# RMSNorm with every row written twice: eight rows per partition in one load, each row normalised in place and stored by itself, all loads of x and all stores in SyncE's queue

## The chip, the cores and the metric

The kernel runs on one core of a Trainium2 chip. The metric is the device time of one execution in microseconds (us). The time of the kernel before is 245.04 us in the first three runs (244.88 to 245.27). The program uses VectorE (DVE), ScalarE (ACT), GpSimd (POOL), SyncE (SP) and the 16 DMA engines that serve the core. TensorE does nothing.

In a profile the "span" is the time from the first to the last instruction. The device time is 1.7 to 2.0 us longer in all runs of this study.

Some terms. "The page" is the profiler's summary of one execution, in numbered parts. An engine issues a transfer into a queue of its own; the 16 DMA engines carry it out in packets.

## The reference

```python
x: (8, 512, 2048) float32, gamma: (2048,) float32

x_rep = np.repeat(x, 2, axis=1)
rms = np.sqrt((x_rep ** 2).mean(axis=-1, keepdims=True) + 1e-6)
return (x_rep / rms) * gamma          # (8, 1024, 2048) float32
```

There are 4096 rows of 8 KB. Each is read once and written twice, next to each other: 33.6 MB in, 67.1 MB out, 100.7 MB in all.

## The kernel before

A tile is 256 rows: 128 partitions of two rows. The 16 tiles are loaded by SyncE as runs of 16 KB per partition. GpSimd issues two stores per tile, one for each copy. A store moves runs of 8 KB, with a gap of 8 KB between them in memory, where the other copy goes.

```python
K = 2
x_t = x_f.rearrange("(n p k) d -> n p k d", p=P, k=K)
out_t = out_v.rearrange("(n p k) r d -> n p k r d", p=P, k=K)
BUFS = 6                                   # for x_tile and for sq_tile
# ... gamma by SyncE, then broadcast to 128 partitions by GpSimd
for i in range(ntiles):
    x_tile = xin.tile([P, K, D], f32)
    nc.sync.dma_start(out=x_tile[:], in_=x_t[i])
    # ... ScalarE: square with row sums, square root; VectorE: reciprocal
    y_tile = sq_tile
    for k in range(K):
        nc.vector.tensor_scalar_mul(out=y_tile[:, k, :], in0=x_tile[:, k, :],
                                    scalar1=rstd[:, k : k + 1])
    nc.vector.tensor_mul(out=y_tile[:], in0=y_tile[:], in1=gamma_kd)
    for r in range(R):
        nc.gpsimd.dma_start(out=out_t[i, :, :, r, :], in_=y_tile[:])
```

Of the kernel before, what the change touches and what calls it, by code (L numbers as in the profile page):

```python
# [1 line left out]

# [4 lines left out]


@with_exitstack  # L10
def kernel(
    ctx: ExitStack,
    tc: tile.TileContext,
    x: bass.AP,
    gamma: bass.AP,
    out: bass.AP,
):
    nc = tc.nc
    P = nc.NUM_PARTITIONS

    B, S, D = x.shape
    Bo, So, Do = out.shape
    R = So // S
    assert D == Do and B == Bo and So == S * R
    eps = 1e-6

    x_f = x.rearrange("b s d -> (b s) d")
    N = B * S
    K = 2
    assert N % (P * K) == 0  # L30
    ntiles = N // (P * K)
    x_t = x_f.rearrange("(n p k) d -> n p k d", p=P, k=K)

    out_v = out.rearrange("b (s r) d -> (b s) r d", r=R)
    out_t = out_v.rearrange("(n p k) r d -> n p k r d", p=P, k=K)

    BUFS = 6
    singles = ctx.enter_context(tc.tile_pool(name="singles", bufs=1))
    xin = ctx.enter_context(tc.tile_pool(name="xin", bufs=BUFS))
    sq = ctx.enter_context(tc.tile_pool(name="sq", bufs=BUFS))  # L40
    small = ctx.enter_context(tc.tile_pool(name="small", bufs=8))

    gamma_b = singles.tile([P, D], mybir.dt.float32)
    nc.sync.dma_start(out=gamma_b[0:1, :], in_=gamma.partition_broadcast(1))
    nc.gpsimd.partition_broadcast(out_ap=gamma_b[:], in_ap=gamma_b[0:1, :])  # L45
    gamma_kd = bass.AP(
        tensor=gamma_b.tensor,
        offset=gamma_b.offset,
        ap=[gamma_b.ap[0], [0, K], gamma_b.ap[1]],
    )  # L50

    eps_t = singles.tile([P, 1], mybir.dt.float32)
    nc.vector.memset(eps_t, eps)  # L53

    inv_d = 1.0 / float(D)

    for i in range(ntiles):
        x_tile = xin.tile([P, K, D], mybir.dt.float32, name="x_tile")
        nc.sync.dma_start(out=x_tile[:], in_=x_t[i])

        sq_tile = sq.tile([P, K, D], mybir.dt.float32, name="sq_tile")
        ss = small.tile([P, K], mybir.dt.float32, name="ss")
        for k in range(K):
            nc.scalar.activation(  # L64
                out=sq_tile[:, k, :],
                in_=x_tile[:, k, :],
                func=mybir.ActivationFunctionType.Square,
                accum_out=ss[:, k : k + 1],
            )

        rms = small.tile([P, K], mybir.dt.float32, name="rms")
        nc.scalar.activation(  # L72
            out=rms[:],
            in_=ss[:],
            func=mybir.ActivationFunctionType.Sqrt,
            scale=inv_d,
            bias=eps_t[:],
        )
        rstd = small.tile([P, K], mybir.dt.float32, name="rstd")
        nc.vector.reciprocal(out=rstd[:], in_=rms[:])  # L80

        y_tile = sq_tile
        for k in range(K):
            nc.vector.tensor_scalar_mul(  # L84
                out=y_tile[:, k, :], in0=x_tile[:, k, :], scalar1=rstd[:, k : k + 1]
            )
        nc.vector.tensor_mul(out=y_tile[:], in0=y_tile[:], in1=gamma_kd)  # L87

        for r in range(R):
            nc.gpsimd.dma_start(out=out_t[i, :, :, r, :], in_=y_tile[:])  # L90


# [1 line left out]
_INS = ['x', 'gamma']  # L94
_OUTS = [((8, 1024, 2048), 'float32')]


# [23 lines left out]
```

## Time and profile before

Part 2 of the page of the kernel before: busy tenths in 40 equal slices of the span (9 is 90% or more), and under them what the DMA engines moved in each slice.

```profile
DVE  0069999950900049680095709577595600000000
ACT  2598656006000150600615061541624000000000
POOL 4003223411010101110130111111121111000000
DMA  6999999999999999999999999999999999999993
GB/s 222 431 431 431 391 433 429 436 417 442 422 431 430 433 422 431 429 427 430 425 430 450 410 426 426 430 425 430 429 425 418 418 417 419 430 417 425 417 426 160
```

The DMA row is 9 from the second slice to the last but one, at about 430 GB/s. No compute row is. A change of the compute can save nothing here unless it also changes what the DMA engines do, or when they start and stop.

Part 5 of the same page, the costliest groups: line, engine, operation, tiles and shapes, count, then busy us and mean ns of one, then the idle time before them with its releaser.

```profile
L64 ACT ACTIVATE sq_tile<-x_tile 128x2048 f32<-128x2048 f32 x32 | 60.8, 1901 | 114.1 <-DMA out_dram<-sq_tile 101.1
L87 DVE TENSOR_TENSOR sq_tile<-sq_tile,gamma_b 128x4096 f32<-128x4096 f32 x16 | 70.8, 4422 | 0.5
L90 POOL DMA_DIRECT2D out_dram<-sq_tile x32 | 27.7, 867 | 169.3 <-DMA out_dram<-sq_tile 125.6
L84 DVE TENSOR_SCALAR sq_tile<-x_tile,rstd 128x2048 f32<-128x2048 f32 x32 | 40.2, 1298 | 0.5
```

ScalarE and GpSimd idle because buffers and earlier stores have not come free: they wait for the DMA engines, not the other way round.

The trace also records every DMA packet with its queue, size, start and duration. At any time about 16 packets run in these records, one for each engine, so "per engine" below is the sum of all durations divided by 16. Durations in a table like this are sums and means over those records; "excess" is what a group of packets took above the median packet of its size.

| kernel before | value |
|---|---|
| first x packet starts | 2.10 us |
| 2048 load packets of 16 KB: median, mean, per engine | 611 ns, 622 ns, 79.6 us |
| 8192 store packets of 8 KB: median, mean, per engine | 309 ns, 311 ns, 159.3 us |
| last store packet ends | 240.57 us |
| span ends | 243.03 us |

This is the DMA row of the transfers between 236 and 246 us, in 40 slices of 0.25 us:

```profile
DMA  9899998999934533000000000000000000000000
```

The engines do not all stop together. The row falls from the twelfth slice on; the last packet ends at 240.57 us. The 16 landings of the last store are spread over 1.81 us. From the last packet to the end of the span there are another 2.46 us.

### The profile page before, as it was taken

The page shows a single profiled execution, that of the slowest core. Times are in us where ns is not written, and L with a number is a line of the kernel's source. Part 1 is how long each engine was busy: PE and PEld are TensorE (multiplying, and loading weights), DVE is VectorE, ACT ScalarE, POOL GpSimd, SP SyncE. Part 2 cuts the span into 40 slices and gives each one's busy share as a digit, 9 for nine tenths or more (in the row PEclk, how much of TensorE's full clock was granted, in tenths as well). Part 3 has the DMA queues.
Part 4 walks back from the last instruction along what each step waited for, and adds up shares of the span by engine and source line. Part 5 has one row for each costly group of instructions (what it writes and reads, how often), then busy time and mean ns, then how long its engine had stood idle before and what let it go on. Part 6 is the DMA issues. An engine that isn't in the chain of part 4 may idle for free.

```text
span 243.0 us, 320 instructions
## 1 busy us (share of the span) xinstructions
DVE 112.7 (46%) x65; ACT 69.5 (29%) x82; POOL 30.2 (12%) x37
## 2 busy tenths in 40 slices
DVE  0069999950900049680095709577595600000000
ACT  2598656006000150600615061541624000000000
POOL 4003223411010101110130111111121111000000
DMA  6999999999999999999999999999999999999993
GB/s 222 431 431 431 391 433 429 436 417 442 422 431 430 433 422 431 429 427 430 425 430 450 410 426 426 430 425 430 429 425 418 418 417 419 430 417 425 417 426 160
DMA packets 11012, 100.69 MB, mean 414 GB/s; under 512 B 769, under 2 KB 769, under 8 KB 769
## 3 DMA queue, kind: packets, MB, share of 16 engines
q0 software_dynamic: 8704, 67.11, 65.7%
q1 hardware_dynamic: 2306, 33.56, 32.8%
q14 instruction: 2, 0.02, 0.0%
HBM read 33.56 MB, written 67.11 MB: 414 GB/s over the span
## 4 chain that ended last, share of the span: by engine, by line
DMA 50%; another core or an unknown queue 15%; issue 4%; ACT 3%; DVE 2%; POOL 1%; POOLq 0%; ACTq 0%
DMA out_dram<-sq_tile 50%; ACT sq_tile L64 3%; DVE sq_tile L87 2%; POOL out_dram L90 1%; POOLq L116 0%; ACT rms L72 0%; DVE rstd L80 0%; ACTq L64 0%; POOLq L90 0%
## 5 line engine op out<-in xcount | busy, mean ns | idle before, releaser
L64 ACT ACTIVATE sq_tile<-x_tile 128x2048 f32<-128x2048 f32 x32 | 60.8, 1901 | 114.1 <-DMA out_dram<-sq_tile 101.1
L87 DVE TENSOR_TENSOR sq_tile<-sq_tile,gamma_b 128x4096 f32<-128x4096 f32 x16 | 70.8, 4422 | 0.5
L90 POOL DMA_DIRECT2D out_dram<-sq_tile x32 | 27.7, 867 | 169.3 <-DMA out_dram<-sq_tile 125.6
L84 DVE TENSOR_SCALAR sq_tile<-x_tile,rstd 128x2048 f32<-128x2048 f32 x32 | 40.2, 1298 | 0.5
L80 DVE RECIPROCAL rstd<-rms 128x2 f32<-128x2 f32 x16 | 2.6, 163 | 77.8 <-ACT rms L72 77.8
L64 ACT ACTIVATION_READ_ACCUMULATOR sq_tile<-x_tile 128x1 f32 x32 | 6.0, 186 | 0.0
L72 ACT ACTIVATE rms<-ss,eps_t 128x2 f32<-128x2 f32 x16 | 4.7, 296 | 0.5
L45 POOL PARTITION_BROADCAST gamma_b<-gamma_b x1 | 2.3, 2293 | 2.1 <-DMA gamma_b<-in_gamma_dram 2.1
L64 ACT ACT_TABLE_LOAD x1 | 1.3, 1283 | 0.7 <-PEq L105 0.7
L72 ACT ACT_TABLE_LOAD x1 | 1.3, 1283 | 0.0
L53 DVE MEMSET eps_t<- 128x1 f32 x1 | 0.1, 59 | 0.8 <-PEq L105 0.8
L105 POOL MEMSET const-float32-0.0<- 128x1 f32 x1 | 0.1, 99 | 0.2 <-issue 0.2
L105 POOL MEMSET const-uint8-127<- 128x1 uint8 x1 | 0.1, 103 | 0.0
L105 POOL MEMSET const-bfloat16-1.0<- 128x1 bf16 x1 | 0.1, 102 | 0.0
L105 POOL MEMSET const-float32-1.0<- 128x1 f32 x1 | 0.1, 99 | 0.0
## 6 DMA issues: line engine op xcount, KB each, us to landing
out_dram<-sq_tile POOLq DMA_DIRECT2D x32, 2048.0 KB, 40.7
x_tile<-in_x_dram SPq DMA_DIRECT2D x16, 2048.0 KB, 24.4
gamma_b<-in_gamma_dram SPq DMA_DIRECT2D x1, 8.0 KB
```

Source lines behind the costliest of these rows:

```text
L45: nc.gpsimd.partition_broadcast(out_ap=gamma_b[:], in_ap=gamma_b[0:1, :])
L53: nc.vector.memset(eps_t, eps)
L64: nc.scalar.activation(out=sq_tile[:, k, :], in_=x_tile[:, k, :], func=mybir.ActivationFunctionType.Square, accum_out=ss[:, k : k + 1],)
L72: nc.scalar.activation(out=rms[:], in_=ss[:], func=mybir.ActivationFunctionType.Sqrt, scale=inv_d, bias=eps_t[:],)
L80: nc.vector.reciprocal(out=rstd[:], in_=rms[:])
L84: nc.vector.tensor_scalar_mul(out=y_tile[:, k, :], in0=x_tile[:, k, :], scalar1=rstd[:, k : k + 1])
L87: nc.vector.tensor_mul(out=y_tile[:], in0=y_tile[:], in1=gamma_kd)
L90: nc.gpsimd.dma_start(out=out_t[i, :, :, r, :], in_=y_tile[:])
L105: nc = _bacc.Bacc("TRN2", target_bir_lowering=False, num_devices=1)
```

## The change

Its intent: fewer and longer load packets (eight rows, 64 KB, per partition); one fused VectorE operation in place, so that no second big buffer is needed; a store for each row as soon as it is ready, with both copies in one transfer, the source repeated by a step of zero; and no use of GpSimd's queue.

```diff
-    K = 2
+    K = 8
-    BUFS = 6
+    BUFS = 3
 ...        (also cut: the new views x_t and out_t, the list xs of loaded tiles)
+    def load(i, parts=1):
+        xt = xin.tile([P, K, D], f32, name="xt")
+        step = K // parts
+        for k in range(0, K, step):
+            nc.sync.dma_start(out=xt[:, k : k + step, :], in_=x_t[i, :, k : k + step, :])
+    def repeated(row):
+        p, d = row.ap
+        return bass.AP(tensor=row.tensor, offset=row.offset, ap=[p, [0, R], d])
+
+    load(0, parts=K // 2)
-    nc.sync.dma_start(out=gamma_b[0:1, :], in_=gamma.partition_broadcast(1))
+    nc.scalar.dma_start(out=gamma_b[0:1, :], in_=gamma.partition_broadcast(1))
 ...
+    for i in range(1, BUFS):
+        load(i)
     for i in range(ntiles):
 ...        (square and square root per row, the squares thrown away in PSUM)
-            nc.vector.tensor_scalar_mul(out=y_tile[:, k, :], in0=x_tile[:, k, :], ...)
-        nc.vector.tensor_mul(out=y_tile[:], in0=y_tile[:], in1=gamma_kd)
-        for r in range(R):
-            nc.gpsimd.dma_start(out=out_t[i, :, :, r, :], in_=y_tile[:])
+            nc.vector.scalar_tensor_tensor(
+                out=xt[:, k, :], in0=xt[:, k, :], scalar=rstd[:], in1=gamma_b[:],
+                op0=Alu.mult, op1=Alu.mult)
+            nc.sync.dma_start(out=out_t[i, :, k], in_=repeated(xt[:, k, :]))
+            if k == K // 2 and 1 <= i and i + BUFS - 1 < ntiles:
+                load(i + BUFS - 1)
```

There are now four tiles of 1024 rows. SyncE's program is: four loads of two rows, two loads of eight rows, 13 stores, the last load, 19 stores.

More of the change, by code (lines that the diff above doesn't have):

```diff
@@ L19 @@
     P = nc.NUM_PARTITIONS
+    f32 = mybir.dt.float32
+    Act = mybir.ActivationFunctionType
+    Alu = mybir.AluOpType
     B, S, D = x.shape
@@ L23 @@
     R = So // S
-    assert D == Do and B == Bo and So == S * R
+    assert R == 2 and D == Do and B == Bo and So == S * R
     eps = 1e-6
-    x_f = x.rearrange("b s d -> (b s) d")
+    inv_d = 1.0 / float(D)
+    K = 8
     N = B * S
-    K = 2
     assert N % (P * K) == 0
     ntiles = N // (P * K)
-    x_t = x_f.rearrange("(n p k) d -> n p k d", p=P, k=K)
-    out_v = out.rearrange("b (s r) d -> (b s) r d", r=R)
-    out_t = out_v.rearrange("(n p k) r d -> n p k r d", p=P, k=K)
-    BUFS = 6
+    x_t = x.rearrange("b s d -> (b s) d").rearrange("(n p k) d -> n p k d", p=P, k=K)
@@ L38 @@
+    out_t = out.rearrange("b s d -> (b s) d").rearrange("(n p k r) d -> n p k r d", p=P, k=K, r=R)
+    BUFS = 3
     singles = ctx.enter_context(tc.tile_pool(name="singles", bufs=1))
     xin = ctx.enter_context(tc.tile_pool(name="xin", bufs=BUFS))
-    sq = ctx.enter_context(tc.tile_pool(name="sq", bufs=BUFS))
+    junk = ctx.enter_context(tc.tile_pool(name="junk", bufs=1, space=bass.MemoryType.PSUM))
     small = ctx.enter_context(tc.tile_pool(name="small", bufs=8))
-    gamma_b = singles.tile([P, D], mybir.dt.float32)
@@ L44 @@
-    nc.sync.dma_start(out=gamma_b[0:1, :], in_=gamma.partition_broadcast(1))
-    nc.gpsimd.partition_broadcast(out_ap=gamma_b[:], in_ap=gamma_b[0:1, :])
-    gamma_kd = bass.AP(
-        tensor=gamma_b.tensor,
-        offset=gamma_b.offset,
-        ap=[gamma_b.ap[0], [0, K], gamma_b.ap[1]],
-    )
-    eps_t = singles.tile([P, 1], mybir.dt.float32)
+    xs = []
+    def load(i, parts=1):
[3 more added lines that the diff above has]
+            nc.sync.dma_start(out=xt[:, k : k + step, :], in_=x_t[i, :, k : k + step, :])
+        xs.append(xt)
@@ L53 @@
+    def repeated(row):
+        p, d = row.ap
+        return bass.AP(tensor=row.tensor, offset=row.offset, ap=[p, [0, R], d])
+    load(0, parts=K // 2)
+    gamma_b = singles.tile([P, D], f32, name="gamma_b")
+    nc.scalar.dma_start(out=gamma_b[0:1, :], in_=gamma.partition_broadcast(1))
+    nc.gpsimd.partition_broadcast(out_ap=gamma_b[:], in_ap=gamma_b[0:1, :])
+    eps_t = singles.tile([P, 1], f32, name="eps_t")
     nc.vector.memset(eps_t, eps)
-    inv_d = 1.0 / float(D)
+    for i in range(1, BUFS):
+        load(i)
@@ L57 @@
     for i in range(ntiles):
-        x_tile = xin.tile([P, K, D], mybir.dt.float32, name="x_tile")
-        nc.sync.dma_start(out=x_tile[:], in_=x_t[i])
-        sq_tile = sq.tile([P, K, D], mybir.dt.float32, name="sq_tile")
-        ss = small.tile([P, K], mybir.dt.float32, name="ss")
+        xt = xs[i]
         for k in range(K):
-            nc.scalar.activation(
-                out=sq_tile[:, k, :],
-                in_=x_tile[:, k, :],
-                func=mybir.ActivationFunctionType.Square,
-                accum_out=ss[:, k : k + 1],
-            )
@@ L71 @@
-        rms = small.tile([P, K], mybir.dt.float32, name="rms")
-        nc.scalar.activation(
-            out=rms[:],
-            in_=ss[:],
-            func=mybir.ActivationFunctionType.Sqrt,
-            scale=inv_d,
-            bias=eps_t[:],
-        )
-        rstd = small.tile([P, K], mybir.dt.float32, name="rstd")
-        nc.vector.reciprocal(out=rstd[:], in_=rms[:])
-        y_tile = sq_tile
-        for k in range(K):
-            nc.vector.tensor_scalar_mul(
-                out=y_tile[:, k, :], in0=x_tile[:, k, :], scalar1=rstd[:, k : k + 1]
-            )
@@ L87 @@
-        nc.vector.tensor_mul(out=y_tile[:], in0=y_tile[:], in1=gamma_kd)
-        for r in range(R):
-            nc.gpsimd.dma_start(out=out_t[i, :, :, r, :], in_=y_tile[:])
+            sq = junk.tile([P, D], f32, name="sq")
+            ss = small.tile([P, 1], f32, name="ss")
+            nc.scalar.activation(out=sq[:], in_=xt[:, k, :], func=Act.Square, accum_out=ss[:])
+            rms = small.tile([P, 1], f32, name="rms")
+            nc.scalar.activation(out=rms[:], in_=ss[:], func=Act.Sqrt, scale=inv_d, bias=eps_t[:])
@@ L94 @@
+            rstd = small.tile([P, 1], f32, name="rstd")
+            nc.vector.reciprocal(out=rstd[:], in_=rms[:])
+            nc.vector.scalar_tensor_tensor(
+                out=xt[:, k, :], in0=xt[:, k, :], scalar=rstd[:], in1=gamma_b[:],
+                op0=Alu.mult, op1=Alu.mult,
+            )
+            nc.sync.dma_start(out=out_t[i, :, k], in_=repeated(xt[:, k, :]))
+            if k == K // 2 and 1 <= i and i + BUFS - 1 < ntiles:
+                load(i + BUFS - 1)
 _INS = ['x', 'gamma']
```

## The prediction

> **What bounds the kernel now.** The 16 DMA engines. On the page, the DMA row of the 40 slices reads 9 in all but the first (6) and the last (3), at about 430 GB/s. VectorE is 46% busy, ScalarE 29%, GpSimd 12%; the longest wait (GpSimd's stores for earlier stores, 125.6 us) is that of an engine with slack. The Trainium skill, "DMA: Bandwidth & Descriptors", section "Where 436 GB/s comes from", gives a ceiling of 435.2 GB/s per core; this trace's 430 agrees. At it the 100.66 MB take 231.3 us (an estimate), 12 us less than the span of 243.0.
>
> From the packet records of the trace: a 16 KB load packet takes 611 ns in the median, 622 in the mean (670 in the first 12 us); an 8 KB store packet 309 ns, 311 in the mean (314 after 180 us). So 8 KB more costs 302 ns, and a packet about 7 ns by itself. Per engine, 128 load packets make 79.6 us and 512 store packets 159.3 us: 238.9 us, which with 2.1 us of start is about the span to the last packet (240.6 us).
>
> **What the change does.**
> - The bytes stay. The zero step on the source saves no read and no write.
> - Tiles 1 to 3 load in 64 KB runs: estimate 8 x 302 + 7 = 2423 ns per packet against 4 x 611, 0.5 us saved; about 1 us with less disturbance where stores begin (load packets of 647 ns near 24 us).
> - Stores: the source row is 8 KB, so I expect 8 KB packets of 309 ns again: 158.2 us, about 0.5 us saved at the end.
> - gamma moves to ScalarE's queue, so the first load is issued 0.4 us earlier.
> - VectorE: one pass (estimate 2.2 us, half of the 4.42 us of 4096 elements) replaces 1.29 + 2.21 us per row: 113 to about 77 us busy. ScalarE, with a square root per row: 70 to about 77 us. GpSimd loses 27.7 us. None of it is on the critical path.
>
> **Order on the one queue.** Loads and stores all go on SyncE's queue. Loads 0 to 2 (25 MB) run alone to about 60 us; only then stores start. The last load waits for tile 0's stores (about 99 us), with five stores (24 us) still queued, so the DMA engines should not run dry; tile 3 loads from about 124 to 144 us, its stores ready long before their turn.
>
> **Sum.** 245.0 - 1.0 - 0.5 - 0.4: about 243.0 us (-0.8%), range 240.5 to 246.5. Faster by over 2%: 0.05; within: 0.88; slower: 0.07.
>
> **What would show it.** DMA row at 9 throughout; 64 KB load packets near 2.42 us; 8 KB store packets near 309 ns; no stores before about 58 us, then no loads until about 124 us; the last packet at about 238.5 us; VectorE down a third.
>
> **What would make it wrong.** (1) The queue running dry around the last load (a dip near 100 to 125 us). (2) Slower packets from the new addresses: stores stride 128 KB between partitions instead of 32 KB, loads 64 KB instead of 16 KB; the same skill page, section "Latency and other measured facts", has copies losing rate at power-of-two row pitches from 512 KiB; no run here shows it yet. (3) Stores as 16 KB packets: about 2 us faster. (4) A longer uneven end.

## More of the kernel before

A "landing" is the report of one DMA engine that its share of a transfer is done, so a store has 16 landings. The time between the first and the last of them is called their spread.

## The result, and the profile after

The changed kernel takes 243.11 us in the median of four runs (243.08 to 243.29), the kernel before 245.00 us beside it. The ratio is 0.9924, with a 95% interval of 0.991 to 0.9938. All runs named here were fast ones, except two of a candidate below that are marked there.

So the change saves 1.9 us, 0.8%, as predicted. The interesting part is that the sum was right by luck: one of its terms had the wrong sign, and a gain that it left out made up for most of that.

Part 2 of the page of the changed kernel:

```profile
DVE  0099920699999900000000001999100000000000
ACT  2699500999699200000000005993000000000000
POOL 4000000000000000000000000000000000000000
DMA  7999989899899999999998998999999999999996
GB/s 273 429 431 431 521 347 521 347 521 347 341 429 425 430 431 426 427 429 427 425 501 347 521 347 350 426 430 426 427 431 425 429 429 429 426 427 427 427 422 269
```

This needs a careful eye. The page counts a packet in the slice in which it starts, and a 64 KB packet lasts 2.42 us of a slice of 6.04 us. So where loads run (slices 5 to 10 and 21 to 24) the row shows 521 and 347 by turns, and some eights, although the records have 16 packets running throughout, from 4 to 238 us. The values at the end of each load phase (341, and 347 with 350) are real in part, as is shown below.

VectorE's and ScalarE's work is now in three blocks. It hurries ahead while loads run, then has to wait for the last load. The groups that answer to those shown of before (part 5):

```profile
L71 ACT ACTIVATE sq<-xt 128x2048 f32<-128x2048 f32 x32 | 59.7, 1865 | 89.8 <-DMA xt<-in_x_dram 89.8
L76 DVE SCALAR_TENSOR_TENSOR xt<-xt,rstd,gamma_b 128x2048 f32<-128x2048 f32 x32 | 75.3, 2352 | 1.8 <-DVE rstd L75 0.7
```

The fused operation takes 2352 ns, against 1298 for the multiplication by the row's factor and half of 4422 for gamma: VectorE's busy time goes from 112.7 to 78.0 us. GpSimd's 27.7 us of store issues are gone.

The same stretches of both kernels, by the view of windows. Columns: stretch and its length, busy us and instructions of DVE, ACT and POOL, TensorE clock, DMA share, GB/s. First the kernel before, then the changed kernel:

```profile
62.00:100.00 38.00, 16.52 (x8) 6.86 (x8) 3.09 (x4) 1.00 1.01 432
100.00:122.00 22.00, 7.93 (x6) 5.71 (x8) 1.36 (x2) 1.00 1.00 425
200.00:236.00 36.00, 0.00 (x0) 0.00 (x0) 0.68 (x1) 1.00 1.01 421
```

```profile
62.00:100.00 38.00, 21.66 (x17) 17.61 (x24) 0.00 (x0) 1.00 1.01 428
100.00:122.00 22.00, 0.00 (x0) 0.00 (x0) 0.00 (x0) 1.00 1.01 428
200.00:236.00 36.00, 0.00 (x0) 0.00 (x0) 0.00 (x0) 1.00 1.01 427
```

Between 100 and 122 us, where the only load of the second half waits for the first tile's stores, the changed kernel keeps its DMA engines full: the feared dry stretch is not there. In the last 36 us of stores it moves 427 GB/s where the kernel before moved 421.

The end of the changed kernel, DMA row from 236 to 246 us:

```profile
DMA  9979999899995300000000000000000000000000
```

The packets of the stores stop near 240.1 us, half a microsecond earlier than before, and more evenly: the 16 landings of the last store are spread over 0.98 us instead of 1.81. The span ends at 241.52 us, so the end after the last packet is 1.43 us, against 2.46 us.

Now the loads. The view of DMA transfers gives, for a stretch, the packets of a queue, their MB, and the time that they took as a share of 16 engines. These two stretches hold the last packet but one of each engine before the stores begin (55.46 to 57.88 us), and the last one (57.88 to 61.45 us):

```profile
DMA packets 16, 1.05 MB, mean 433 GB/s; under 512 B 0, under 2 KB 0, under 8 KB 0
q1 hardware_dynamic: 16, 1.05, 100.1%
```

```profile
DMA packets 16, 1.05 MB, mean 294 GB/s; under 512 B 0, under 2 KB 0, under 8 KB 0
q1 hardware_dynamic: 16, 1.05, 98.6%
```

In the first, 100.1% of 2.42 us is 2.42 us per packet. In the second, 98.6% of 3.57 us is 3.52 us per packet, for the same 64 KB. So at the place where the one queue turns from loads to stores, each engine's last load packet takes 1.1 us longer. The same happens at 142.6 to 143.1 us, at the end of the last load (0.97 us per engine). Nothing later gives this back: the store packets that follow take their usual 309 ns.

| | before | changed |
|---|---|---|
| first x packet starts, us | 2.10 | 1.74 |
| load packets, per engine, us | 79.6 | 80.3 (16 KB: 20.2; 64 KB: 60.1) |
| of it excess at the start / where stores begin after loads, us | 0.89 / 0.48 | 0.61 / 1.10 and 0.97 |
| store packets, per engine, us | 159.3 | 158.7 |
| last store packet ends, us | 240.57 | 240.09 |
| end of span after that, us | 2.46 | 1.43 |
| span, us | 243.03 | 241.52 |

The terms per engine are means over 16 engines, while the slowest engine ends the kernel, so they need not add up to the difference to 0.1 us. The profiled execution of the changed kernel was the slowest of its four; the others have spans of 241.3 us, 1.7 us less than the kernel before.

The landings show where the gain lies. Load and store packets together take 238.9 us per engine before and 239.0 us after. The 16 landings of the last store come at 239.78 us in the mean before, and at 239.74 us after. So the average DMA engine was done no earlier. The 1.5 us by which the span is shorter are the lag of the last landing behind that mean (1.11 us before, 0.68 us after) and the time from the last landing to the end (2.14 and 1.09 us).

### The profile page after: what moved, and what is told of

Read it like the earlier page. It is cut to its first block, busy times and chain, and to the rows that moved or that the text cites. A ratio compares the mean times of both kernels' runs of the same rounds, so it can differ in the third digit from the quotient of the medians.

```text
span 241.5 us, 318 instructions
## 1 busy us (share of the span) xinstructions
DVE 78.0 (32%) x65; ACT 73.1 (30%) x98; POOL 2.5 (1%) x5
## 4 chain that ended last, share of the span: by engine, by line
DMA 48%; DVE 10%; ACT 7%; issue 3%; another core or an unknown queue 1%; SPq 1%; DVEq 0%
DMA xt<-in_x_dram 35%; DMA out_dram<-xt 13%; DVE xt L76 10%; ACT sq L71 6%; SPq L50 1%; ACT rms L73 0%; DVE rstd L75 0%; DVEq L76 0%
## 5 line engine op out<-in xcount | busy, mean ns | idle before, releaser
L71 ACT ACTIVATE sq<-xt 128x2048 f32<-128x2048 f32 x32 | 59.7, 1865 | 89.8 <-DMA xt<-in_x_dram 89.8
L76 DVE SCALAR_TENSOR_TENSOR xt<-xt,rstd,gamma_b 128x2048 f32<-128x2048 f32 x32 | 75.3, 2352 | 1.8 <-DVE rstd L75 0.7
L75 DVE RECIPROCAL rstd<-rms 128x1 f32<-128x1 f32 x32 | 5.0, 157 | 89.4 <-ACT rms L73 89.4
L73 ACT ACTIVATE rms<-ss,eps_t 128x1 f32<-128x1 f32 x32 | 9.4, 294 | 1.0
L71 ACT ACTIVATION_READ_ACCUMULATOR sq<-xt 128x1 f32 x32 | 6.0, 186 | 0.0
```

The lines of the kernel that those rows point to most:

```text
L71: nc.scalar.activation(out=sq[:], in_=xt[:, k, :], func=Act.Square, accum_out=ss[:])
L73: nc.scalar.activation(out=rms[:], in_=ss[:], func=Act.Sqrt, scale=inv_d, bias=eps_t[:])
L75: nc.vector.reciprocal(out=rstd[:], in_=rms[:])
L76: nc.vector.scalar_tensor_tensor(out=xt[:, k, :], in0=xt[:, k, :], scalar=rstd[:], in1=gamma_b[:], op0=Alu.mult, op1=Alu.mult,)
```

## The experiments

Twelve kernels were run. All gave the right result. In their names, "turn" means the place in one queue where stores follow loads.

### 1. Is it the long runs, and does the turn depend on them? (r16)

```diff
-    def load(i, parts=1):
+    def load(i, parts=4):
```

> The changed kernel with every tile loaded as four 16 KB runs per partition, nothing else. Theory 1 (what a 64 KB packet saves is lost at the two places where the queue turns from loads to stores, because the last load packet of each engine stretches there, from 2.42 to about 3.5 us, and the stretch grows with the packet): load packets of 611 ns, stretch at each turn at most 0.5 us per engine instead of 1.05, so 243.1 + 0.6 - 1.2 = about 242.5 us, a ratio to the kernel before of 0.990. Theory 2 (the turn costs the same 1.05 us whatever the packet): 243.1 + 0.6 = 243.7 us, 0.9945. Theory 3 (64 KB runs are what made the changed kernel faster): 244.5 us or more, 0.998.

243.72 us (243.60 to 243.83), ratio 0.9944. The number is that of theory 2, but the packets say something between. The excess at the two turns is 0.67 and 0.65 us per engine, spread over the last two packets or so of each engine. That is less than the 1.10 and 0.97 us with 64 KB, and far more than a quarter of it. The load packets take 80.3 us per engine in all, as with 64 KB: the long runs save 0.6 us of packet overhead and lose about as much again at the turns. What the trace shows for the 0.6 us by which this kernel is slower is its last engine: after the second turn the 16 landings of a store are spread over 1.9 us (1.2 us in the changed kernel), and still 1.48 us at the end (0.98). My theory 1 falls as stated. The turn costs something with either size.

### 2. GpSimd's queue in the changed kernel (pool)

```diff
-            nc.sync.dma_start(out=out_t[i, :, k], in_=repeated(xt[:, k, :]))
+            nc.gpsimd.dma_start(out=out_t[i, :, k], in_=repeated(xt[:, k, :]))
```

> The changed kernel with its stores issued by GpSimd, as before, nothing else. Theory (about 1 us of the gain is the end of the program: with stores on GpSimd's queue, GpSimd's closing drain ends only about 1.4 us after the last landing, against 0.2 us for the barrier without it): the time from the last store packet to the end of the span goes from 1.4 back to about 2.4 us, store packets after 180 us may average 314 ns again, and the time is 244 to 245 us. Rival (the end is shorter because SyncE finds its waits already met, whoever issues): the end stays at 1.4 to 1.6 us.

247.01 us, ratio 1.0076: slower than the kernel before, and 2 us more than expected. Its DMA row from 236 to 246 us:

```profile
DMA  9989999999999556463333200100000000000000
```

The end after the last packet is 2.47 us, as the theory said. The rest I had not expected. The engines part: the row falls over about 3.4 us, and the 16 landings of the last store are spread over 3.31 us; the spread had grown from 1.4 us at 137 us to 2.0 us at 143 us and 3.8 us at 204 us. The store packets take 160.0 us per engine instead of 158.7. So stores in GpSimd's queue go with uneven engines here, even more than in the kernel before; why more was not tested. The run also puts loads and stores into two queues. That is not what makes it slow: the same kernel with ScalarE in GpSimd's place takes 242.37 us (experiment 8).

### 3. The zero step (two)

```diff
-            nc.sync.dma_start(out=out_t[i, :, k], in_=repeated(xt[:, k, :]))
+            for r in range(R):
+                nc.sync.dma_start(out=out_t[i, :, k, r], in_=xt[:, k, :])
```

> The changed kernel with two stores per row instead of one with the source repeated by a zero step. Theory (the zero step only saves instructions; packets are 8 KB either way): the same time within 0.3 us, 64 store issues of 1 MB, 8192 packets of 309 ns. Rival (storing both copies side by side is what took away the slow packets of 314 ns late in the kernel before): about 0.5 to 1 us slower, with late store packets of 314 ns in the mean.

243.07 us, ratio 0.9921: the same. 8192 packets of 309 ns, 158.5 us per engine. The zero step is neither gain nor loss; neither is it the cause of the even late stores.

### 4. The fused operation (twopass)

```diff
-            nc.vector.scalar_tensor_tensor(... op0=Alu.mult, op1=Alu.mult)
+            nc.vector.tensor_scalar_mul(out=xt[:, k, :], in0=xt[:, k, :], scalar1=rstd[:])
+            nc.vector.tensor_mul(out=xt[:, k, :], in0=xt[:, k, :], in1=gamma_b[:])
```

> The changed kernel with the fused VectorE operation split again into two passes. Theory (VectorE is off the critical path): VectorE busy goes from 78 to about 117 us and the time stays within 0.2 us of 243.1. Rival (part of the gain comes from the shorter VectorE work): up to 1 us slower.

242.97 us (242.75 to 243.36), ratio 0.9916: the same. VectorE is busy for 113.1 us instead of 78.0 (about 117 were expected). Its work is off the path, in either form.

### 5. The earlier start (gsync)

```diff
-    load(0, parts=K // 2)
 ...
-    nc.scalar.dma_start(out=gamma_b[0:1, :], in_=gamma.partition_broadcast(1))
+    nc.sync.dma_start(out=gamma_b[0:1, :], in_=gamma.partition_broadcast(1))
+    load(0, parts=K // 2)
```

> The changed kernel with gamma's load put back on SyncE's queue, ahead of the first load of x. Theory (0.4 us of the gain is the earlier start): first x packet at about 2.1 instead of 1.74 us, time 243.5 us, ratio to the kernel before 0.994. Rival (the start is hidden): no change, 243.1 us.

243.02 us (242.95 to 243.10), ratio 0.9916: no change, the rival is right. The trace shows where the 0.36 us goes. The first x packet starts at 2.10 us, and the landings are 0.3 to 0.5 us late up to the store that lands at 126.9 us (126.4 in the changed kernel). The next landing, that of the last load, comes at 147.1 us in this kernel and at 147.3 us in the changed one. The turn at the end of that load cost 0.85 us per engine here and 0.97 there, and left landings spread over 0.75 and 1.20 us. A start that is 0.36 us earlier is less than what one turn varies by; this rests on one trace of each kernel.

### 6. What in GpSimd's queue lengthens the end? (gpool)

```diff
-    nc.scalar.dma_start(out=gamma_b[0:1, :], in_=gamma.partition_broadcast(1))
+    nc.gpsimd.dma_start(out=gamma_b[0:1, :], in_=gamma.partition_broadcast(1))
```

> The changed kernel with only gamma's load issued by GpSimd; the stores stay with SyncE. It asks what in GpSimd's queue lengthens the end. Theory A (GpSimd's drain waits for late landings of its own queue): one early transfer costs nothing at the end, 1.4 us from last packet to end of span, about 243.1 to 243.5 us (gamma is later at hand, which delays nothing on the DMA engines). Theory B (any use of GpSimd's queue makes the closing drain long): end about 2.4 us, 244.1 us.

243.22 us (242.76 to 243.74), ratio 0.9924. The DMA row from 236 to 246 us, and a span that ends at 241.4 us:

```profile
DMA  9899999989995200000000000000000000000000
```

The end after the last packet is 1.50 us: theory A. One early, small transfer from GpSimd costs nothing at the end; 32 stores up to the end do. Whether their lateness or their number counts was not tested apart. The traces show where the time goes. The closing of the program has two steps that matter here: GpSimd waits in an instruction called drain, and then all engines meet at a barrier. In the kernel before, the last store lands at 240.89 us. SyncE, which in the closing of the program waits for the last store first, passes its nine waits one after the other by 241.5 us. But GpSimd's closing drain, begun at 201.2 us, ends only at 242.25 us, 1.36 us after the landing, and the closing barrier waits for it. In this experiment the drain that GpSimd comes to after its last work is over at 9.7 us. In the changed kernel the last store lands at 240.42 us and the barrier begins at 240.60 us.

### 7. The queue alone (bact)

```diff
-            nc.gpsimd.dma_start(out=out_t[i, :, :, r, :], in_=y_tile[:])
+            nc.scalar.dma_start(out=out_t[i, :, :, r, :], in_=y_tile[:])
```

This is the kernel before with one word changed.

> The kernel before with its stores issued by ScalarE instead of GpSimd, nothing else. Theory (the queue alone gives about 1 us at the end, and the slow late packets belong to GpSimd's stores): end of span 1.4 instead of 2.5 us after the last packet, late store packets 309 ns, 16 KB and 8 KB packets otherwise as before, no stretch of load packets beyond 0.5 us per engine; 243.0 to 243.6 us, that is nearly all that the whole change gives. Risk: ScalarE stands still at its stores and the DMA engines run dry, which would show as a dip in the DMA row and a time above 245 us. Rival (the gain is in the order of the transfers and the long runs): 244.5 to 245 us.

242.03 us (241.81 to 242.11), ratio 0.9877: not most of what the change gives but more than all of it, by 1.1 us. Its DMA row from 236 to 246 us, in a span that ends at 240.0 us:

```profile
DMA  8999989973000000000000000000000000000000
```

The end after the last packet is 1.27 us. The engines stop together: the landings of the last store are spread over 0.54 us instead of 1.81. The store packets take 158.4 us per engine instead of 159.3. And the loads, in runs of 16 KB, take 79.4 us per engine against 80.3 in the changed kernel: there is an excess of 0.37 us where stores first begin, and none after it. In this kernel loads and stores lie in two queues, and while both have work their packets alternate one for one (in the stretch from 30 to 40 us, 175 load packets and 173 store packets). ScalarE, which now waits at its stores, did not let the DMA engines run dry. Split as above for the changed kernel, the 3.0 us of span are 1.0 us in the mean of the last store's landings (238.77 us), 0.8 us in the lag of the last one (0.33 us), and 1.2 us after it (0.94 us).

### 8. Two queues in the changed kernel (aact)

```diff
-            nc.sync.dma_start(out=out_t[i, :, k], in_=repeated(xt[:, k, :]))
+            nc.scalar.dma_start(out=out_t[i, :, k], in_=repeated(xt[:, k, :]))
```

> The changed kernel with its stores issued by ScalarE instead of SyncE, so that loads and stores lie in two queues again, neither of them GpSimd's; nothing else. Theory (what the change loses is lost where its one queue turns from loads to stores, about 0.9 us per engine at each of two turns; two queues have no such turns): the stretched load packets after the first store disappear, 64 KB packets average at most 2450 ns instead of 2506, and the time is 241.3 to 242 us, ratio 0.985 to 0.988. Rival (the turns cost nothing in the end, or belong to 64 KB loads as such): 243 us, 0.992. Risk: ScalarE waits in order and the DMA engines run dry, to be seen in the DMA row; then it tells nothing of turns.

242.37 us (242.34 to 242.49), ratio 0.9889; 64 KB packets average 2453 ns. The time lies between the theory's (241.3 to 242) and the rival's (243). The stretch at the end of the first three tiles' loads is gone (0.03 us per engine); where stores first begin, at 16 to 24 us, the 16 KB load packets have about 0.55 us of excess. The stretch at the end of the last load is still there (0.76 us per engine, at 124.4 to 125.3 us). It can't be said that loads ran alone there. These are the transfers between 108 and 124 us, q1 with the loads and q10 with the stores:

```profile
q1 hardware_dynamic: 96, 6.29, 90.7%
q10 hardware_dynamic: 96, 0.77, 11.4%
```

The two queues alternate packet for packet, 96 for 96. Since a load packet has 64 KB and a store packet 8 KB, the load gets nearly all of the bytes while a store waits in the other queue. So the theory holds in part: two queues took away one of the two stretches, all load packets together take 79.5 us per engine instead of 80.3, and the time falls by 0.7 us. "Two queues have no such turns" is wrong, and what makes the stretch is not known: in experiment 2, where 64 KB loads and 8 KB stores of two queues also alternate, it is 0.15 us at the end of the last load. This run also had slow late store packets (0.60 us of excess per engine after 200 us), without GpSimd's queue. Their cause stays open.

### 9. One more turn (b2)

```diff
-    BUFS = 3
+    BUFS = 2
```

> The changed kernel with two tile buffers instead of three, so that the one queue turns three times from loads to stores instead of twice, and twice back instead of once. Theory (each turn to stores costs 0.75 to 1.05 us per engine, each turn back 0.2 to 0.35): three groups of stretched load packets, 243.1 + 1.0 to 1.4 = about 244.3 us, ratio 0.997. Rival (the stretch is only how the packets are recorded and is given back later): 243.1 us, 0.992. A dip of the DMA row to under 9 between turns would mean that the queue ran dry, and the run would not decide.

244.07 us in the median, but from 243.43 to 245.09, ratio 0.9964. The three turns are there, with 1.26, 0.89 and 0.49 us of excess per engine, and so are the two turns back (0.23 and 0.12 us of excess on the store packets there). The engines never ran dry. All six runs are slower than all of the changed kernel's, so the direction is as the theory has it. The size is less sure: the median rises by 1.0 us, but in the traced run (243.91 us) the three turns add up to 2.64 us against 2.07 for the two of the changed kernel, 0.6 us more where 1.0 to 1.4 were expected. A turn's cost varies by as much as half of it, and the time with it.

### 10. A first candidate: stores of 32 KB runs (dup)

A packet has about 9 ns of its own by these records: eight store packets of 309.9 ns (the mean) less one 64 KB packet of 2418 ns leave 61 ns for seven packets; with the median of 309 ns it is 8 ns. So here VectorE writes each row twice, side by side, and a store moves both copies of two rows as one run.

```diff
+        y = yout.tile([P, K, R, D], f32, name="y")          # K = 2, three buffers
-                out=xt[:, k, :], in0=xt[:, k, :], scalar=rstd[:], in1=gamma_b[:],
+                out=y[:, k, :, :], in0=repeated(xt[:, k, :]), scalar=rstd[:], in1=repeated(gamma_b[:]),
-            nc.sync.dma_start(out=out_t[i, :, k], in_=repeated(xt[:, k, :]))
+        nc.sync.dma_start(out=out_t[i], in_=y[:])
```

Loads are of 16 KB runs, six by SyncE and the others by ScalarE.

> A candidate to beat both: two rows per partition, VectorE writes each normalised row twice side by side, so that a store is one contiguous 32 KB run per partition; loads of 16 KB runs on ScalarE's queue after the first six, stores on SyncE's. Theory (time is packets times their time, and each packet has about 9 ns of its own): 32 KB store packets of about 1213 ns, 128 x 1.213 = 155.3 us per engine instead of 158.7, loads 79.6 us, no stretch at turns since two queues alternate; 1.7 + 79.6 + 155.3 - 0.9 to the last packet, about 235.7 us, time about 239.0 us, ratio 0.975. VectorE about 150 us busy, off the path. If larger store packets are no better than four of 8 KB: 242 us or more.

The four fast runs took 245.79 to 247.90 us (median 247.03), ratio 1.0076; two more, of 249.57 and 250.50 us, count as slow. A miss. The packets are as expected (1213 ns; 155.6 us per engine for stores, 80.0 for loads), but the engines run dry late:

```profile
195.00:205.00 10.00, 10.00 (x3) 0.00 (x0) 0.00 (x0) 1.00 0.48 206
```

Half of 10 us is lost, while VectorE is busy. The order of VectorE's instructions in the trace shows a cause, which no run with another order has tested: the two reciprocals of the last tile stand ahead of the multiplications of the last four tiles, three of which are long loaded by then. The last load lands at 189.2 us; VectorE waits for it until 193.9 us, and only then begins eight operations of 4.5 us, with a single store in flight, which lands at 198.9 us. I took the large buffers or the unequal packets of loads and stores for the cause when I wrote what I expected of the next two candidates; the trace does not bear that out.

### 11. A second candidate: stores of 16 KB runs (best1)

Loads by SyncE in 16 KB runs as in the kernel before, stores by ScalarE, one row per store, six buffers each way. The first lines are those of the first candidate:

```diff
+            y = yout.tile([P, 1, R, D], f32, name="y")      # six buffers
+                out=y[:, 0, :, :], in0=repeated(xt[:, k, :]), scalar=rstd[:], in1=repeated(gamma_b[:]),
-            nc.sync.dma_start(out=out_t[i, :, k], in_=repeated(xt[:, k, :]))
+            # issued after the next row's ScalarE work
+            nc.scalar.dma_start(out=out_t[i, :, k : k + 1], in_=y[:])
```

> A second candidate: two queues as in the kernel before (loads of 16 KB runs by SyncE, stores by ScalarE), each normalised row written twice side by side by VectorE and stored as one 16 KB run per partition, one store per row, six buffers each way. Theory (packets times their time, no turns, no GpSimd queue, and the dry stretch of the first candidate came of its three large store buffers): store packets of 611 ns, 256 x 0.611 = 156.4 us per engine, loads 79.4 us, last packet at about 236.9 us, time 240.0 to 240.5 us, ratio 0.98. If the DMA row dips, the loads are again issued too late: 242 us or more.

240.51 us (240.33 to 240.62), ratio 0.9812: the best, 4.5 us less than the kernel before and 2.6 us less than the changed one. Part 2 of its page:

```profile
DVE  0099899529916527266763757737899899870000
DMA  7999999999999999999999999999999999999996
GB/s 251 423 431 387 439 439 434 417 423 439 439 437 423 422 431 439 439 434 415 426 439 439 437 417 419 439 439 437 428 420 428 439 437 434 420 423 439 437 437 277
```

Store packets of 611 ns take 156.5 us per engine (158.7 in the changed kernel), loads 79.5 us. The loads have next to no excess after 40 us. VectorE is busy for 146.4 us, nearly twice the 78.0 of the changed kernel, and the DMA row stays at 9 all the same. The kernel also differs from experiment 7 in its order and its fused operation, so not all of the 1.5 us between the two need come from the longer packets; the store packets alone account for 2.0 us per engine.

### 12. 32 KB both ways (best3)

```diff
-    K = 2
+    K = 4
-    BUFS = 6
+    BUFS = 3
-            y = yout.tile([P, 1, R, D], f32, name="y")      # six buffers
+            y = yout.tile([P, 2, R, D], f32, name="y")      # three buffers
```

> The second candidate with 32 KB packets both ways: four rows per tile in three buffers, loads of one 32 KB run per partition (the first in two halves), each store two rows of two copies, 32 KB, in three buffers. Theory (a packet has about 9 ns of its own, so 64 load and 128 store packets per engine instead of 128 and 256 save 1.7 us; loads and stores of one packet size alternate one to one, so loads run ahead, unlike in the first candidate, where a 16 KB load packet alternated with a 32 KB store packet): last packet at about 235.7 us, time about 238.9 us, ratio 0.975. If the three large buffers alone made the first candidate run dry, the DMA row dips again and the time is 242 us or more.

243.04 us (240.75 to 243.14), ratio 0.9899: another miss. Load packets take 79.3 us and store packets 155.4 us per engine, as expected, and 15 of the 16 landings of the last store are there by 236.8 us. The sixteenth comes at 239.9 us. One engine had fallen behind, and the whole kernel then waits for it. One execution of six (240.75 us) was nearly 2.3 us faster than the median; no trace of it exists, so whether all engines kept up in that one is not known. Why one engine falls behind was not settled.

## Why the prediction was right, point by point

- **The bound: right.** The DMA engines were full before and after. Halving VectorE's passes, undone in experiment 4, is worth nothing.
- **The packets: right.** 64 KB load packets of 2423 ns were predicted, their median is 2418; 8 KB store packets of 309 ns were predicted and measured.
- **The order on the one queue: right.** Stores start at 61.5 us ("about 60"), the last load runs from 125.7 to 147 us ("about 124 to 144"), and the queue does not run dry.
- **"the last packet at about 238.5 us": wrong.** It ended at 240.09 us, 0.5 us earlier than before and not 2 us. The prediction placed all of its gain before the last packet. Most of it came after.
- **"about 1 us with less disturbance where stores begin": wrong, in sign.** The load packets take 0.7 us more per engine, not 1.0 us less. The 0.6 us of overhead that longer runs save is there, and the start is 0.3 us better. But the one queue turns from loads to stores twice, and at each turn the last load packets stretch by about 1 us per engine; the kernel before had 0.48 us of that in all. I had seen the disturbance in the trace of before, and wrote that it would become less. It became more (experiments 1, 8 and 9 vary it).
- **Stores, "about 0.5 us saved at the end": right.** 159.3 to 158.7 us per engine. The queue alone gives as much (158.4 us in experiment 7).
- **"the first load is issued 0.4 us earlier": true, but no gain in time came of it** (experiment 5).
- **The end of the program: left out.** I took the 2.4 us after the last packet as fixed. With the stores out of GpSimd's queue it is 1.43 us (2.47 with them put back, 1.50 with only an early transfer there, 1.27 with the kernel before and ScalarE's queue). I counted GpSimd's 27.7 us as off the path and did not ask what its queue does when the program closes.

So a gain of 1.0 us that I did not see stands in for the 1.7 us of load gain that did not come; the rest, as far as the records show, is in the engines ending more evenly (0.98 us of spread for 1.81). That the total agreed to 0.1 us is luck; the sum behind it was not right.

What is shown: that the issuing queue of the stores is the part of the change that pays (experiments 2, 7 and 8), and that one queue for loads and stores, in this order, gives about 0.7 us back (experiment 8; 1.1 us in experiment 7, which differs in more). That the stretched load packets are what costs this time fits experiments 8 and 9, but is in part argued. What stays open: why load packets stretch when stores follow; why a turn's cost varies from 0.5 to 1.3 us; why store packets late in some runs take 2% longer; and why single engines fall behind.

## What to carry to other kernels

When a kernel keeps all DMA engines full, count packets times their time, then look at three places that a busy share does not show: the turn from loads to stores, the spread of the engines' ends, and the time from the last packet to the end of the program. Try the queue that issues the stores by itself before a rewrite: here one word gave 3.0 us, and the rewrite 1.9. Where a compute engine has time to spare, let it lay out data so that packets are longer (one of three candidates gained by it), but read in the compiled order of the instructions that no early work waits behind a late load.

## What the Trainium skill lacked or had wrong

- "DMA: Bandwidth & Descriptors", section "Issuing engines are not separate DMA queues", says that issuing from several engines "will only save the time on the sequencer it takes to initiate the DMA". Here the same transfers took 242.37 us in two queues against 243.11 us in one, in another order, with the DMA engines full in both. Where the one queue goes from loads to stores, the last load packets of each engine take 0.5 to 1.3 us longer; with two queues one of the two stretches was gone and the other still 0.76 us. No page has that.
- The same page, section "SWDGE vs HWDGE vs iDMA", compares the two kinds of queue in set-up and in features. It lacks that stores in GpSimd's queue up to the end of a program lengthen its end: 2.46 and 2.47 us after the last packet with them, 1.18 to 1.50 us in all twelve kernels without.
- The same page, section "Latency and other measured facts", says that DMA engines 7 and 15 are usually slower, and puts that down, as a guess, to GpSimd's queue. The traces here do not name engines. Uneven engines did come with GpSimd's queue: the landings of the last store were spread over 1.81 and 3.31 us with it, and over 0.54 us with the kernel before and ScalarE's. But eight of these 16 landings came within 0.5 us (0.3 us in experiment 2) and the other eight after them, so more than two engines lagged. And one engine fell 3.1 us behind in a kernel whose transfers all came from SyncE and ScalarE (experiment 12).
- The warning about power-of-two row pitches in that section starts at 512 KiB. At 64 KB (loads) and 128 KB (stores) between partitions no loss was seen: 8 KB store packets took 309 ns with the old and the new addresses.
- The ceiling of 435.2 GB/s in the section "Where 436 GB/s comes from" was borne out: 64 KB packets of 2418 ns on 16 engines are 434 GB/s. The same section says that for transfers between HBM and the on-chip memory the HBM side, at about 358 GB/s, is the limit; that figure is half of what two cores share, and this program, on one core, moved 414 GB/s over the whole span in the kernel before and 422 in that of experiment 11.
